# Matrix product with layer norm: the opening takes column quarter 2 of B first

## The chip, the cores and the metric

The kernel runs on one core of one Trainium2 chip. Its time is the device time of one execution in microseconds (us), median of several runs. A profile shows one execution on five engines: TensorE (PE; its weight loads are a row of their own, PEld), VectorE (DVE), ScalarE (ACT), GpSimd (POOL) and SyncE (SP), which here only issues DMA transfers, in the order of its queue. The *span* is the time from the first to the last instruction of the profiled execution.

## The reference

```python
x = np.matmul(a, b)                       # a, b: 2048 x 2048 float32
mean = np.mean(x, axis=-1, keepdims=True)
var = np.var(x, axis=-1, keepdims=True)
normalized = (x - mean) / np.sqrt(var + eps)
return (gamma * normalized + beta).astype(np.float32)
```

A matrix product whose rows are normalised and then scaled and shifted by two vectors. The kernel multiplies in fp16 and adds up in fp32.

## The kernel before, in words

**Tiles.** The output has 16 row blocks of 128 rows. Its 2048 columns are cut into four column quarters of 512; one quarter of one row block fills one of the eight PSUM banks. The inner dimension has 16 k-tiles of 128. One product is a 128x128 block of A (transposed, as the weights) by a 128x512 block of B, and there are 16 x 4 x 16 = 1024 of them, all issued by `mm` (line 85). All of B is kept in SBUF as fp16 in `b16`, k-tile by k-tile, with the four quarters side by side.

**Why there is an opening.** B comes in as float32 in the course of the kernel, so the first R = 5 row blocks are worked on together while it arrives. For these rows a quarter is not finished at once. It is summed over the k-tiles that are there, the partial sum is copied out of PSUM into the row's buffer `xs` by ScalarE (`put_aside`, line 264), and later partial sums are added to it by VectorE (`add_part`, line 268; `add_rest`, line 272, which also takes the statistics of the quarter). Three quarters are put aside early, in the order given by `ASIDE`; the fourth is `MAIN`, quarter 3.

**The order of work in the opening** is written out by hand, since the kernel is scheduled manually: each engine runs its instructions in program order.

- Loads: the list `arrivals` (line 163) interleaves five blocks of A (rows 0 to 4, k-tiles 0 to 3) and four blocks of B (`load_b1`, one k-tile of the first aside quarter each), 256 KB apiece. Then come 512 KB blocks of two k-tiles (`load_b2`): the other two aside quarters for k-tiles 0 to 3, the main quarter for k-tiles 0 to 11 mixed with more of A, then k-tiles 4 to 11 of the first aside quarter and 4 to 7 of quarter 1. All are issued by SyncE into one pool of six staging buffers and cast to fp16 by VectorE.
- Products: `filler` matmuls on zeros (line 245) keep TensorE busy until data are there; `turn` (line 247) transposes blocks of A on TensorE and copies them out with ScalarE. Then follow the first aside quarter for k-tiles 0 to 3, the second and third (line 302), the main quarter for k-tiles 0 to 11, and after that `part` for each quarter's remaining k-tiles: the first aside quarter k-tiles 4 to 11, the second and third k-tiles 4 to 15, the main one 12 to 15, and last the first aside quarter's 12 to 15.
- The rest of B's loads stand in the list `later` (line 354), cast by ScalarE. After the last load of the third aside quarter, and after the last of the list, a small GpSimd copy (`gate`, line 362) holds GpSimd's queue back, on which whole rows of A for the blocks from 5 on are loaded (`load_row`, line 343). SyncE then turns these with transposing DMAs (`turn_ahead`, line 347).
- `close_opening` (line 459) adds the very last partial sums of each opening row, works out mean and deviation (`stats`, line 100) and queues the row's normalising in two pieces, columns 0 to 1023 and 1024 to 2047 (`queue_norm`, line 130). These pieces are done by VectorE, one after each quarter of the later rows (`drain`).

**The rest.** Row blocks 5 to 15 go quarter by quarter in the order 0, 1, 2, 3, sixteen products each (`quarter`, line 449). The last row has its own ending (`finish_row`, line 400).

Of the kernel before, what the change touches and what calls it, by code (L numbers as in the profile page):

```python
# [16 lines left out]
def kernel(  # L17
# [9 lines left out]
    nc = tc.nc  # L27
    P = 128
# [4 lines left out]
    n_kt = K // P  # L33
    NB = 512
    n_nb = N // NB
    NH = N // 2
    KC = 4
    KW = KC * P
    n_kc = n_kt // KC
    R = 5  # L40
    ASIDE, MAIN = (0, 1, 2), 3
    assert n_kt % KC == 0 and n_nb == 4 and n_mt > R + 2

    if isinstance(eps, bass.AP):
# [21 lines left out]
    b16 = bpool.tile([P, n_kt, N], FP16)  # L66
# [6 lines left out]
    def bank(name):  # L73
        return psum.tile([P, NB], FP32, tag="ps", name=name)
# [4 lines left out]
    def at(i):  # L79
        return pair[i // 2][:, i % 2]  # L80

    def mm(i, q, kt, first, last):
        if (i, q) not in acc:
            acc[i, q] = bank(f"acc{i}_{q}")
        nc.tensor.matmul(  # L85
            acc[i, q], at(i)[:, kt, :], b16[:, kt, ds(q * NB, NB)],
            start=first, stop=last,
        )
# [81 lines left out]
    def half_stage():  # L170
        n = fresh["st"]
        if n % 2 == 0:
            held["st"] = stg.tile([P, 2, NB], FP32, tag="st", name=f"st{n // 2}")
        fresh["st"] += 1
        return held["st"][:, n % 2, :]
# [19 lines left out]

    def load_b1(k):
        st = half_stage()
        nc.sync.dma_start(st, b[ts(k, P), 0:NB])  # L198
        nc.vector.tensor_copy(b16[:, k, 0:NB], st)  # L199

    def load_b2(k, q, cast=nc.vector.tensor_copy):
        st = stg.tile([P, 2, NB], FP32, tag="st", name=f"stb{q}_{k}")
        nc.sync.dma_start(
            st, b[ds(k * P, 2 * P), ds(q * NB, NB)].rearrange("(t p) n -> p t n", p=P))
        cast(b16[:, k:k + 2, ds(q * NB, NB)], st)  # L205
        return st
# [3 lines left out]
    def load_pair(j, c):  # L210
        if len(pairs[j]) == 2:
            load_a2(pairs[j][0], c)
        else:
            load_a1(pairs[j][0], c)

    for what in arrivals:
        (load_a1(what[1], 0) if what[0] == "a" else load_b1(what[1]))
# [4 lines left out]
    K3 = n_kt - KC  # L222
    for c in range(n_kc - 1):
# [4 lines left out]
        if c + 2 < n_kc:  # L228
            if c > 0:
                load_pair(1, c + 1)  # L230
            load_pair(2, c + 1)
    load_b2(KC, 0)
    load_b2(KC + 2, 0)
    for j in range(len(pairs)):
        load_pair(j, n_kc - 1)
        if j < 2:
            load_b2(2 * KC + 2 * j, 0)
    load_b2(KC, 1)
    load_b2(KC + 2, 1)

# [2 lines left out]
    def filler(n, to=None):  # L243
        for _ in range(n):
            nc.tensor.matmul(warm if to is None else to, zeros[:, 0:P], zeros, start=True, stop=True)  # L245

    def turn(rows, c):
        n = len(rows)
        t_ps = psum.tile([P, n, KC, P], FP16, tag="ps", name=f"tps{rows[0]}_{c}")
        for m, i in enumerate(rows):  # L250
            for j in range(KC):
                nc.tensor.transpose(t_ps[:, m, j, :], a16_of[i, c][:, ts(j, P)], ident)  # L252
        i0 = rows[0]
        nc.scalar.copy(  # L254
            pair[i0 // 2][:, ds(i0 % 2, n), ds(c * KC, KC), :], t_ps)

    def turn_last(i):
        nc.sync.dma_start_transpose(at(i)[:, ds(K3, KC), :], a16_of[i, n_kc - 1])

    def put_aside(p, q):  # L260
        if xs[p] is None:
            xs[p] = xpool.tile([P, N], FP32, tag="x", name=f"x{p}")
            bnst[p] = stat.tile([P, n_nb, 6], FP32, tag="bnst", name=f"bnst{p}")
        nc.scalar.copy(xs[p][:, ds(q * NB, NB)], acc.pop((p, q)))  # L264
# [11 lines left out]
    filler(9)  # L276
    turn([0], 0)
    filler(3)
    mm(0, 0, 0, True, False)
    filler(1)  # L280
    turn([1], 0)
    filler(2)
    for i in range(2, R - 1):
        turn([i], 0)
        mm(i - 1, 0, 0, True, False)
    for p in range(R - 2):
        mm(p, 0, 1, False, False)
    for kt in (0, 1):
        mm(R - 2, 0, kt, kt == 0, False)
    for p in range(R - 2):  # L290
        mm(p, 0, 2, False, False)
    turn([R - 1], 0)
    mm(R - 2, 0, 2, False, False)
    for p in range(R - 1):
        mm(p, 0, 3, False, True)
        put_aside(p, 0)
    for kt in range(KC):
        mm(R - 1, 0, kt, kt == 0, kt == KC - 1)
    put_aside(R - 1, 0)


    for q in ASIDE[1:]:
# [8 lines left out]
    def part(q, k0, k1, k_row, done):  # L311

        for kt in range(k0, k_row):
            for p in range(R):
                mm(p, q, kt, kt == k0, False)
        for p in range(R):
            for kt in range(k_row, k1):
                mm(p, q, kt, kt == k0, kt == k1 - 1)
            done(p, q)
# [23 lines left out]
    def load_row(i):  # L343
        a16[i] = a16p.tile([P, K], FP16, tag="a16", name=f"a16_{i}")
        nc.gpsimd.dma_start(a16[i], a[ts(i, P), :])  # L345
# [6 lines left out]


    later = [(k, 1) for k in range(2 * KC, n_kt, 2)]
    later += [(k, 2) for k in range(KC, n_kt, 2)]
    later += [(k, q) for q in (MAIN, 0) for k in range(K3, n_kt, 2)]
    for n, (k, q) in enumerate(later):
        for i in {0: (0,), 1: (1,), 2: (2,), 4: (3, 4)}.get(n, ()):
            turn_last(i)
        st = load_b2(k, q, nc.scalar.copy)  # L360
        if (k, q) in ((n_kt - 2, 2), later[-1]):
            nc.gpsimd.tensor_copy(gate, st[:, 0, 0:1])
        if (k, q) == (n_kt - 2, 2):
            load_row(R)
    turn_ahead(R)


    part(0, KC, K3, K3 - 2, add_part)
    part(1, KC, n_kt, K3, add_rest)
    part(2, KC, n_kt, K3, add_rest)  # L370
    nc.sync.dma_start(gamma_b, gamma.unsqueeze(0).to_broadcast([P, N]))
    nc.sync.dma_start(beta_b, beta.unsqueeze(0).to_broadcast([P, N]))
    if eps_ap is not None:
# [87 lines left out]
        queue_norm(p, *stats(p))  # L461

    part(MAIN, K3, n_kt, K3, add_rest)
    part(0, K3, n_kt, K3, close_opening)
    for i in range(R, n_mt):
        last = i == n_mt - 1
        turn_ahead(i + 2)
# [49 lines left out]
```

## Time and profile before

| | |
|---|---|
| median of three runs | 244.88 us (243.92, 244.88, 245.12) |
| the profiled execution's own time | 245.38 us |
| its span, mean granted TensorE clock | 242.9 us, 0.994 |
| products (line 85) | 1024, 379 ns each in the records (they overlap), 223.0 us busy |
| VectorE casts of B | 4 of 256 KB at 0.43 us, 16 of 512 KB at 0.69 us |
| ScalarE casts of B | 14 of 512 KB at 1.04 us |
| ScalarE copies of partial sums (line 264) | 20 at 0.61 us |
| VectorE sums (lines 268, 272) | 5 and 20 at 0.68 us |
| HBM read, written | 35.67 MB, 16.78 MB |

A line of the profile names the program line and engine, the operation, the tile written and the tiles read, and the busy time. An arrow `<-` after an idle time names what ended it. The line `DMA` of the profile's slices gives the busy share of the core's 16 DMA engines in tenths in 40 equal slices of the span, and `GB/s` what they moved. A matmul's recorded duration is longer than the distance to the next one, because matmuls overlap; the distance is had from the chain of waits, which merges a run of them into one line with a count. The chain is followed back from the last instruction to what released it, and shown here in order of time.

### The profile page before, as it was taken

Reading aid. Unit: us, or ns where it says so; the run is one execution under the profiler, and the core shown is the slowest. Engines: PE = TensorE matmul, PEld = TensorE weight load, DVE = VectorE, ACT = ScalarE, POOL = GpSimd, SP = SyncE. Lnnn points to the kernel's source line nnn. Section 1 sums busy time; section 2 is a strip of 40 time slices with the busy share of each in tenths; the row PEclk is TensorE's granted clock in tenths of the full one; section 3 lists DMA queues with packets and bytes.
Section 4 is the critical chain, followed back from the end, with each engine's and each line's share of the span. In section 5 each row is a group of like instructions: output and inputs, shape, how many; then the busy total and the mean of one; then the engine's idle time right before and its main releaser. Section 6 shows DMA issues by size and latency. Waiting matters only on the chain.

```text
span 242.9 us, 2971 instructions
## 1 busy us (share of the span) xinstructions
PE 234.3 (96%) x1117; PEld 107.2 (44%) x1117; DVE 171.2 (70%) x300; ACT 65.9 (27%) x115; POOL 12.7 (5%) x20
## 2 busy tenths in 40 slices
PE   7899999999999999999999999999999999999992
PEld 2344554344444444444444444444444444444441
DVE  1543554625449998999999999998758292846761
ACT  2376444065750013020201103022111121212132
POOL 0000000000120001000000000005400000000000
PEclk9999999999999999999999999999999999999997
DMA  5999999999979999749899978988907235130405
GB/s 101 391 387 387 385 366 300 275 356 386 385 153 198 350 224 169 233 154 205 248 200 233 254 166 292 245 202 199 260 33 170 89 112 150 47 126 1 173 0 173
DMA packets 43909, 53.28 MB, mean 219 GB/s; under 512 B 27124, under 2 KB 27124, under 8 KB 43640
## 3 DMA queue, kind: packets, MB, share of 16 engines
q1 hardware_dynamic: 42312, 47.34, 62.7%
q0 software_dynamic: 1584, 5.77, 14.5%
q8 instruction: 8, 0.13, 0.2%
q14 instruction: 5, 0.04, 0.0%
HBM read 35.67 MB, written 16.78 MB: 216 GB/s over the span
## 4 chain that ended last, share of the span: by engine, by line
PE 93%; DMA 2%; DVE 1%; ACT 1%; SPq 0%; issue 0%; DVEq 0%
PE acc L85 91%; DMA st<-in_a_dram 2%; PE tps L252 1%; ACT x L442 1%; DVE x L268 1%; DVE bnst L407 0%; PE y L430 0%; DVE a16s L186 0%; PE warm L245 0%; SPq L198 0%; SPq L184 0%; PE ms_ps L425 0%; ACT mv_last L423 0%; DVE mv_last L422 0%; ACT lead L426 0%
## 5 line engine op out<-in xcount | busy, mean ns | idle before, releaser
L85 PE MATMUL acc<-b,at 128*128 128x512 f16 x1024 | 223.0, 379 | 1.5 <-DVE b L199 1.0
L85 PEld LDWEIGHTS <-at 128*128 128x128 f16 x1024 | 99.7, 98 | 120.5 <-issue 1.2
L96 DVE BATCH_NORM_STATS2 bnst<-x 128x6 f32<-128x512 f32 x43 | 29.5, 689 | 23.4 <-ACT x L95 23.4
L117 DVE SCALAR_TENSOR_TENSOR x<-x,rstd,beta_b 128x512 f32<-128x512 f32 x62 | 43.9, 748 | 0.6
L111 DVE SCALAR_TENSOR_TENSOR x<-x,mv,gamma_b 128x512 f32<-128x512 f32 x60 | 43.1, 760 | 0.0
L95 ACT COPY x<-acc 128x512 f32<-128x512 f32 x43 | 24.5, 585 | 66.9 <-PE acc L85 66.7
L272 DVE TENSOR_TENSOR x<-acc,x 128x512 f32<-128x512 f32 x20 | 13.6, 678 | 13.4 <-PE acc L85 13.4
L106 ACT ACTIVATE sq<-ve 128x1 f32<-128x1 f32 x15 | 3.0, 203 | 65.8 <-DVE ve L104 65.8
L205 DVE CAST b<-stb 128x1024 f16<-128x1024 f32 x16 | 11.1, 694 | 13.1 <-DMA stb<-in_b_dram 13.1
L205 ACT CAST b<-stb 128x1024 f16<-128x1024 f32 x14 | 14.6, 1045 | 16.6 <-DMA stb<-in_b_dram 16.6
L273 DVE BATCH_NORM_STATS2 bnst<-x 128x6 f32<-128x512 f32 x20 | 13.9, 694 | 0.7
L264 ACT COPY x<-acc 128x512 f32<-128x512 f32 x20 | 10.2, 610 | 5.7 <-PE acc L85 5.7
L254 ACT COPY at<-tps 128x512 f16<-128x512 f16 (+1 forms) x11 | 8.0, 741 | 13.1 <-PE tps L252 12.9
L345 POOL DMA_DIRECT2D a<-in_a_dram x11 | 6.0, 545 | 92.8 <-DMA at<-a 92.0
L245 PE MATMUL warm<-zeros 128*128 128x512 f16 x19 | 6.5, 476 | 1.2 <-DVE zeros L152 1.2
L186 DVE CAST a16s<-st 128x512 f16<-128x512 f32 x8 | 3.4, 428 | 5.7 <-DMA st<-in_a_dram 5.6
L194 DVE CAST a16s<-sta 128x1024 f16<-128x1024 f32 x6 | 4.2, 694 | 4.1 <-DMA sta<-in_a_dram 4.1
L391 POOL TENSOR_SCALAR gb<-gb 1x1024 f32<-1x1024 f32 x2 | 5.8, 2917 | 0.0
L252 PE MATMUL tps<-ident,a16s 128*128 128x128 f16 x60 | 5.2, 220 | 0.6 <-DVE a16s L186 0.6
L252 PEld LDWEIGHTS <-a16s 128*128 128x128 f16 x60 | 3.9, 98 | 3.9 <-DVE a16s L186 2.2
L102 DVE BATCH_NORM_AGGREGATE mv<-bnst 128x2 f32<-128x24 f32 x15 | 4.0, 264 | 0.5
L245 PEld LDWEIGHTS <-zeros 128*128 128x128 f16 x19 | 2.1, 118 | 4.4 <-issue 2.9
(33 smaller groups left out, 26.3 us busy)
## 6 DMA issues: line engine op xcount, KB each, us to landing
stb<-in_b_dram SPq DMA_DIRECT2D x30, 512.0 KB, 6.8
out_dram<-x SPq DMA_DIRECT2D x30, 512.0 KB, 3.3
a<-in_a_dram POOLq DMA_DIRECT2D x11, 512.0 KB, 6.2
sta<-in_a_dram SPq DMA_DIRECT2D x6, 512.0 KB, 6.5
st<-in_a_dram SPq DMA_DIRECT2D x8, 256.0 KB, 6.5
st<-in_b_dram SPq DMA_DIRECT2D x4, 256.0 KB, 6.6
gamma_b<-in_gamma_dram SPq DMA_DIRECT2D x1, 1024.0 KB, 5.5
beta_b<-in_beta_dram SPq DMA_DIRECT2D x1, 1024.0 KB, 8.3
```

Source lines behind the costliest of these rows:

```text
L85: nc.tensor.matmul(acc[i, q], at(i)[:, kt, :], b16[:, kt, ds(q * NB, NB)], start=first, stop=last,)
L95: nc.scalar.copy(xs[i][:, qs], acc[i, q])
L96: nc.vector.bn_stats(bnst[i][:, q, :], xs[i][:, qs])
L111: nc.vector.scalar_tensor_tensor(xs[i][:, qs], xs[i][:, qs], mv[:, 0:1], gamma_b[:, qs], AluOp.subtract, AluOp.mult)
L117: nc.vector.scalar_tensor_tensor(xs[i][:, qs], xs[i][:, qs], rstd, beta_b[:, qs], AluOp.mult, AluOp.add)
L205: cast(b16[:, k:k + 2, ds(q * NB, NB)], st)
L245: nc.tensor.matmul(warm if to is None else to, zeros[:, 0:P], zeros, start=True, stop=True)
L252: nc.tensor.transpose(t_ps[:, m, j, :], a16_of[i, c][:, ts(j, P)], ident)
L254: nc.scalar.copy(pair[i0 // 2][:, ds(i0 % 2, n), ds(c * KC, KC), :], t_ps)
L264: nc.scalar.copy(xs[p][:, ds(q * NB, NB)], acc.pop((p, q)))
L272: nc.vector.tensor_tensor(xs[p][:, qs], acc[p, q], xs[p][:, qs], AluOp.add)
L273: nc.vector.bn_stats(bnst[p][:, q, :], xs[p][:, qs])
```

## The change

`ASIDE` is turned round from (0, 1, 2) to (2, 1, 0), and a name `Q0` for its first entry replaces the literal 0 wherever the first aside quarter was meant; `ASIDE[2]` replaces the literal 2 in the same way. So in the five opening rows quarter 2 of B is loaded, multiplied and put aside first and closed last, and quarter 0 takes the place that quarter 2 had. Quarters 1 and 3 stay where they were, and so do all rows from 5 on. The four loads of `load_b1` now read columns 1024 to 1535 of B.

```diff
-    ASIDE, MAIN = (0, 1, 2), 3
+    ASIDE, MAIN = (2, 1, 0), 3
+    Q0 = ASIDE[0]
...
     def load_b1(k):
         st = half_stage()
-        nc.sync.dma_start(st, b[ts(k, P), 0:NB])
-        nc.vector.tensor_copy(b16[:, k, 0:NB], st)
+        qs = ds(Q0 * NB, NB)
+        nc.sync.dma_start(st, b[ts(k, P), qs])
+        nc.vector.tensor_copy(b16[:, k, qs], st)
...
-    load_b2(KC, 0)
-    load_b2(KC + 2, 0)
+    load_b2(KC, Q0)
+    load_b2(KC + 2, Q0)
...
-            load_b2(2 * KC + 2 * j, 0)
+            load_b2(2 * KC + 2 * j, Q0)
...
-    mm(0, 0, 0, True, False)
+    mm(0, Q0, 0, True, False)
...
     for p in range(R - 1):
-        mm(p, 0, 3, False, True)
-        put_aside(p, 0)
+        mm(p, Q0, 3, False, True)
+        put_aside(p, Q0)
...
-    later += [(k, 2) for k in range(KC, n_kt, 2)]
-    later += [(k, q) for q in (MAIN, 0) for k in range(K3, n_kt, 2)]
+    later += [(k, ASIDE[2]) for k in range(KC, n_kt, 2)]
+    later += [(k, q) for q in (MAIN, Q0) for k in range(K3, n_kt, 2)]
...
-        if (k, q) in ((n_kt - 2, 2), later[-1]):
+        if (k, q) in ((n_kt - 2, ASIDE[2]), later[-1]):
             nc.gpsimd.tensor_copy(gate, st[:, 0, 0:1])
-        if (k, q) == (n_kt - 2, 2):
+        if (k, q) == (n_kt - 2, ASIDE[2]):
             load_row(R)
...
-    part(0, KC, K3, K3 - 2, add_part)
+    part(Q0, KC, K3, K3 - 2, add_part)
     part(1, KC, n_kt, K3, add_rest)
-    part(2, KC, n_kt, K3, add_rest)
+    part(ASIDE[2], KC, n_kt, K3, add_rest)
...
     part(MAIN, K3, n_kt, K3, add_rest)
-    part(0, K3, n_kt, K3, close_opening)
+    part(Q0, K3, n_kt, K3, close_opening)
```

More of the change, by code (lines that the diff above doesn't have):

```diff
@@ L284 @@
         turn([i], 0)
-        mm(i - 1, 0, 0, True, False)
+        mm(i - 1, Q0, 0, True, False)
     for p in range(R - 2):
-        mm(p, 0, 1, False, False)
+        mm(p, Q0, 1, False, False)
     for kt in (0, 1):
-        mm(R - 2, 0, kt, kt == 0, False)
+        mm(R - 2, Q0, kt, kt == 0, False)
     for p in range(R - 2):
-        mm(p, 0, 2, False, False)
+        mm(p, Q0, 2, False, False)
     turn([R - 1], 0)
-    mm(R - 2, 0, 2, False, False)
+    mm(R - 2, Q0, 2, False, False)
     for p in range(R - 1):
-        mm(p, 0, 3, False, True)
-        put_aside(p, 0)
+        mm(p, Q0, 3, False, True)
+        put_aside(p, Q0)
     for kt in range(KC):
-        mm(R - 1, 0, kt, kt == 0, kt == KC - 1)
-    put_aside(R - 1, 0)
+        mm(R - 1, Q0, kt, kt == 0, kt == KC - 1)
+    put_aside(R - 1, Q0)
     for q in ASIDE[1:]:
```

## The prediction

> **What bounds the kernel now.** I read the page first (busy shares, slices, chain), then the chain in order of time, TensorE's own waits, the timeline of the opening, and DMA rates microsecond by microsecond. The page:
>
> ```profile
> span 242.9 us, 2971 instructions
> PE 234.3 (96%) x1117; PEld 107.2 (44%) x1117; DVE 171.2 (70%) x300; ACT 65.9 (27%) x115; POOL 12.7 (5%) x20
> ...
> PE 93%; DMA 2%; DVE 1%; ACT 1%; SPq 0%; issue 0%; DVEq 0%
> ```
>
> TensorE is busy 96% of the span and makes 93% of the chain that ended last. The chain in order of time (start, duration, what) shows whether it runs without holes:
>
> ```profile
> 1.66 6.00 DMA st<-in_a_dram
> ...
> 9.25 0.39 PE acc L85
> ...
> 12.31 12.73 PE acc L85 x59
> ...
> 46.84 1.29 DVE x L268 x2
> ...
> 48.17 185.79 PE acc L85 x860
> ```
>
> 59 matmuls in 12.73 us are 0.2158 us each, 860 in 185.79 us are 0.2160: one rate over nearly the whole kernel. What TensorE waits for, totalled (us, times, longest):
>
> ```profile
> PE warm L245 <- DVE zeros L152: 1.2, 1, 1.2
> PE acc L85 <- DVE b L199: 1.0, 1, 1.0
> PE tps L252 <- DVE a16s L186: 0.6, 1, 0.6
> PE acc L85 <- DVE x L268: 0.4, 2, 0.2
> ```
>
> Three of these lie in the first 9 us; the last is the 0.4 us at 47 us, where `add_part` gives PSUM banks back. So the time is the opening (9.24 us to the second product), a stream at a fixed rate to 233.97 us, and an 8.9 us tail. A change that keeps the products can act only on the opening, on the stream by opening a hole, or on the tail. In the opening the data come late:
>
> ```profile
> 4.92 0.43 DVE L186 CAST a16s<-st 128x512 f16<-128x512 f32 x1 [3.71 <-DMA st<-in_a_dram]
> 7.01 0.43 DVE L199 CAST b<-st 128x512 f16<-128x512 f32 x1 [1.67 <-DMA st<-in_b_dram]
> 7.69 0.43 DVE L186 CAST a16s<-st 128x512 f16<-128x512 f32 x1 [0.25 <-DMA st<-in_a_dram]
> 8.36 0.43 DVE L186 CAST a16s<-st 128x512 f16<-128x512 f32 x1 [0.25 <-DMA st<-in_a_dram]
> ```
>
> A's first block is cast at 4.92, B's first at 7.01, then one 256 KB block each 0.67 us. The gap of 2.09 us before B's first block is 1.42 us over that pace. The rates (window, length, busy time by engine, clock, DMA share, GB/s):
>
> ```profile
> 2.00:3.00 1.00, 1.00 (x4) 0.43 (x3) 0.00 (x0) 0.02 (x1) 0.00 (x0) 1.00 0.56 190
> 3.00:4.00 1.00, 1.00 (x4) 0.33 (x3) 0.00 (x0) 0.00 (x0) 0.00 (x0) 1.00 0.66 102
> 4.00:5.00 1.00, 0.84 (x3) 0.15 (x1) 0.08 (x1) 0.00 (x0) 0.00 (x0) 1.00 0.91 100
> 5.00:6.00 1.00, 0.59 (x6) 0.43 (x7) 0.35 (x1) 0.16 (x1) 0.00 (x0) 1.00 0.82 176
> 7.00:8.00 1.00, 0.51 (x2) 0.10 (x1) 0.74 (x2) 0.00 (x0) 0.00 (x0) 1.00 1.05 404
> ```
>
> Reads crawl at about 100 GB/s from 3 to 5 us and run at 404 from 7 on. This slow spell is the only place where an address might matter, and the whole question of this case.
>
> **The change part by part.** It renames: in the order of column quarters 2 and 0 change places. I go through what is moved.
>
> *The four first B loads (`load_b1`).* Before and after: four SyncE DMAs of 256 KB, 128 rows of 2048 bytes with 8192 bytes between rows, each followed by a VectorE cast of 0.43 us. Number, size, place in SyncE's queue and in VectorE's order stay; only the start in each row moves from byte 0 to byte 4096. Cost 4 x (0.43 - 0.43) = 0, if the DMA takes as long. No row shows quarter 2 read first, so I bound it: from below by the whole spell vanishing (3 to 6 us moved 102 + 100 + 176 = 378 KB, which at 404 GB/s takes 0.94 us, so -2.06 us), from above by B's first block losing its 1.42 us once more (+1.42). I take 0, by the nearest rows: the blocks cast from 7.69 on come from the same bytes 0 to 2047 of their rows as the two slow ones, and run at the full pace.
>
> *The 512 KB loads (`load_b2`).* The groups for quarter 2 (2 in the opening, 6 in the later list) now read quarter 0 and the other way round (4 and 2, besides the 4 small loads). Casts of 512 KB blocks in the opening follow one another at 13.08, 14.44 (quarter 1), 15.78, 17.14 (quarter 2) and 18.50 (A): 1.36, 1.34, 1.36, 1.36 us, so quarters 1 and 2 and A cost the same. Quarter 0's own small blocks ran at 0.67 us per 256 KB, the same rate again. VectorE casts of 0.69 us and ScalarE casts of 1.04 us stay as many and in the same places, 16 and 14. Cost 0. The cover is thin at the start: B's fourth block is cast from 11.71 to 12.14, and the first product that needs it starts at about 12.37 (one product after 12.15), so 0.2 us is hidden; the first 512 KB block is ready at 13.77 and wanted 8 products later at about 14.1, so 0.3 us. Any delay beyond that goes one for one into the end. In the later list the cover is wide: the block for k-tile 8 of quarter 1 is ready at 49.5 and wanted after 60 products from 47 us, about 60 us; quarter 2's last block is ready at 61.3 and wanted after 68 us.
>
> *The products (`mm`), 80 of quarter 0 and 80 of quarter 2 in the five opening rows.* Same number, same weights, same order of k-tiles and rows, other columns of `b16`. All matmuls of the group last 376 to 389 ns in the records whichever quarter they read, and the spacing is 0.216 us throughout. Cost 0.
>
> *Evacuations and sums (`put_aside`, `add_part`, `add_rest`).* Same engines, same count (ScalarE 20 x 0.61, VectorE 5 x 0.68 and 20 x 0.68 with 20 x 0.69 of statistics), another 2 KB of each row of `xs`. Cost 0.
>
> *The gate copies and the row load behind them.* They follow the third aside quarter and the last load of the list, by place as before: the GpSimd copies (0.18 us) and the first whole-row load on its queue keep their place, and so does the transpose on SyncE behind it. Cost 0.
>
> *The close of the opening rows.* The last quarter that `close_opening` sums is now 2. The work queued behind it begins with columns 0 and 1; that used to follow a fresh sum of quarter 0 and now follows a fresh sum of quarter 2. VectorE runs both in its own order, and between the sum and the first centring (L111, 93.92 us) lie the statistics of all rows (from 84.1 to 92.6), so nothing waits for it. The normalising, its stores and rows 5 to 15 are not touched, nor is the tail. Cost 0; no wait is added anywhere.
>
> Sum 0. The profiled execution took 245.38 us, of which 242.9 are the span and 2.48 lie around it; the median of the three runs is 244.88, 0.50 below it (0.2%). I forecast no change, 244.9 us against the median.
>
> **The rivals.** *The slow spell belongs to the columns (faster).* A's and B's first blocks read bytes 0 to 2047 of rows 0 to 127 of two matrices of the same 16 MB; the two might stand in each other's way, and after the change B's stands 4096 bytes off. Then B's first block lands 0.67 us after A's, at 5.57 instead of 7.0, and each block behind it is 1.42 us earlier. TensorE would follow: the first product could start when the transposed A is copied out (6.42), and the second turn behind it and one filler at about 6.9, against 8.17; the blocks after that hold it back, and they are 1.42 us earlier. Time 244.88 - 1.42 = 243.46; with the whole spell gone 242.8. For it: the spell hits these two blocks. Against it: A's first block was complete at 4.92, so from 5 us on these two no longer meet, and yet 5 to 6 us moves only 176; from 7 on blocks of A and B with the same columns mix at 404. It looks like the age of the kernel or a first contact with the memory, which the change leaves. [...] Chance 0.12.
>
> *The new columns read slowly where the old did not (slower).* Quarter 2 of B's rows meets A's stream or something else at the start, and B's first block loses its 1.42 us a second time. Place: the same gap before the first B cast, at 7 us now. Everything behind it on SyncE's one queue lands later and TensorE with it, because the cover above is only 0.2 us; it decides by the 0.5% from a delay of about 1.4 us on (1.2 us and the cover). Time 244.88 + 1.42 = 246.30. Against it: quarter 2's blocks at 15.78 and 17.14 came at the common pace beside A's. Chance 0.10.
>
> *Waits by span instead of by piece (slower).* A 512 KB cast writes two k-tiles, with other quarters lying between its two pieces. If the program's waits were set by the whole span, the products of k-tile 1 on quarter 2 would wait for the cast of quarter 3, done at 19.85 + 0.69 = 20.54, about 10 us late: 255. Against it: the same span covers k-tile 1 of quarter 0 today, and those products run in the nine from 9.92 us on, before even the first such cast at 13.08. Chance 0.02.
>
> **How the numbers follow.** No change has 0.76: same instructions, same order, same sizes, and full pace from every quarter wherever a row shows it. About 0.5% (1.2 us) is what a measurement of this kernel can tell from no change: the three runs alone spread from 243.92 to 245.12. Of the 0.76 I give 0.01 to each side for that spread. Faster 0.12 + 0.01 = 0.13; slower 0.10 + 0.02 + 0.01 = 0.13; same 0.74. The range reaches from the faster rival's 243.4 to the slower rival's 246.3; the far ends (242.8 and 255) stay out. The forecast's own range is 243.9 to 245.4, the lowest run and the profiled one.
>
> **What would show it.** Right: the casts of A's first and B's first block stand about 2.1 us apart, with about 100 GB/s from 3 to 5 us; 0.67 us between the following casts; 860 products in one piece at 0.216 us; TensorE's waits the same four lines; the last products end near 234 us; the tail 8.9 us. The faster rival shows as a gap of about 0.7 us before the first B cast and a second turn near 6.9 us; the slower as a gap of 3.5 us; the third as a new TensorE wait of 10 us on a VectorE cast of `b` (L205). I am wrong if the first reads depend on their columns, or if a quarter's place in SBUF changes a cast's or a product's duration, which no row hints at.

## The result, and the profile after

The changed kernel took 245.94 us (median of 17 runs, 245.08 to 247.50), the kernel before 244.31 us in as many runs beside it (243.61 to 245.44). The ratio is 1.0069, with a 95% interval of 1.0049 to 1.0089: slower by 1.6 us, a little over the 0.5% that the prediction set as the limit of what can be told. The profiled execution took 245.94 us, with a span of 243.8.

The page of the changed kernel:

```profile
span 243.8 us, 2971 instructions
PE 235.4 (97%) x1117; PEld 107.9 (44%) x1117; DVE 171.2 (70%) x300; ACT 65.9 (27%) x115; POOL 12.7 (5%) x20
...
PE 91%; DMA 4%; SPq 1%; ACT 1%; DVE 1%; issue 0%
```

The number of instructions is the same to the last one and so is the busy time of every engine but TensorE. In the chain, DMA has gone from 2% to 4%. In order of time (start, duration, what) it reads:

```profile
4.02 8.80 DMA st<-in_a_dram
...
13.73 0.22 PE acc L86
...
13.96 12.68 PE acc L86 x58
26.64 0.45 PE tps L254 x8
...
34.70 200.12 PE acc L86 x927
```

The first DMA link of the chain now ends at 12.82 us, with A's fifth block, where it ended at 7.66 with A's second. The unbroken run of products begins at 13.96, where a run longer by one product began at 12.31. The two runs are best compared by their ends, at the next transposes (`tps`). In the kernel before these stand at 25.05, and the products behind the last of them start at 33.11:

```profile
25.05 0.45 PE tps L252 x8
...
33.11 13.61 PE acc L85 x63
```

So TensorE is 1.59 us late at both places (26.64 and 34.70). After that the rate is what it was: 927 products in 200.12 us are 0.2159 us each. TensorE's own waits (us, times, longest) agree:

```profile
PE acc L86 <- DVE b L201: 1.8, 2, 1.0
PE warm L247 <- DVE zeros L153: 1.2, 1, 1.2
PE y L432 <- ACT lead L428: 0.4, 1, 0.4
```

The wait for a cast of B's small blocks has grown from 1.0 to 1.8 us, in two pieces. Where the blocks are late shows in VectorE's casts of the nine 256 KB blocks, which are the first casts of all (start, duration, what, and in brackets the idle time before and what ended it):

```profile
3.96 0.43 DVE L187 CAST a16s<-st 128x512 f16<-128x512 f32 x1 [2.75 <-DMA st<-in_a_dram]
5.28 0.43 DVE L201 CAST b<-st 128x512 f16<-128x512 f32 x1 [0.90 <-DMA st<-in_b_dram]
5.94 0.43 DVE L187 CAST a16s<-st 128x512 f16<-128x512 f32 x1 [0.23 <-DMA st<-in_a_dram]
7.40 0.43 DVE L187 CAST a16s<-st 128x512 f16<-128x512 f32 x1 [1.03 <-DMA st<-in_a_dram]
8.30 0.43 DVE L187 CAST a16s<-st 128x512 f16<-128x512 f32 x1 [0.48 <-DMA st<-in_a_dram]
9.70 0.43 DVE L201 CAST b<-st 128x512 f16<-128x512 f32 x1 [0.97 <-DMA st<-in_b_dram]
11.98 0.43 DVE L201 CAST b<-st 128x512 f16<-128x512 f32 x1 [1.86 <-DMA st<-in_b_dram]
12.85 0.43 DVE L187 CAST a16s<-st 128x512 f16<-128x512 f32 x1 [0.44 <-DMA st<-in_a_dram]
13.48 0.43 DVE L201 CAST b<-st 128x512 f16<-128x512 f32 x1 [0.21 <-DMA st<-in_b_dram]
```

Before, one gap was long (2.09 us, ahead of B's first block) and all others were 0.65 to 0.68. Now the first A block comes 0.96 us earlier and B's first block 1.73 us earlier, and then the train stumbles at five of the blocks behind: over the pace of 0.67 us a block, the eight gaps add up to 13.48 - 3.96 - 8 x 0.67 = 4.16 us, where they added up to 11.71 - 4.92 - 8 x 0.67 = 1.43 before. So the ninth block comes 4.16 - 1.43 - 0.96 = 1.77 us later (13.48 against 11.71), and TensorE is 1.59 us late. The rates (window, length, busy time by engine, clock, DMA share, GB/s) show the same:

```profile
3.00:4.00 1.00, 1.00 (x4) 0.33 (x3) 0.04 (x1) 0.00 (x0) 0.00 (x0) 1.00 0.92 299
5.00:6.00 1.00, 1.00 (x7) 0.71 (x6) 0.49 (x2) 0.32 (x1) 0.00 (x0) 1.00 0.82 190
7.00:8.00 1.00, 1.00 (x9) 0.52 (x8) 0.43 (x1) 0.24 (x1) 0.00 (x0) 1.00 0.85 256
```

Three times the rate of before in the fourth microsecond, but 256 GB/s where it had reached 404.

The two profiled spans differ by only 0.9 us, since the execution profiled before had a hole at 47 us: the four products from 46.72 to 48.17 took 1.45 us instead of 4 x 0.216 = 0.86, because `add_part` came late. The changed kernel, 1.59 us later by then (34.70 against 33.11), does not have it. So 1.59 - 0.59 = 1.00, and the last product ends 0.85 us later (234.82 against 233.97; the remaining 0.15 is the slightly shorter spacing). The tail is 8.9 us before and 9.0 after.

### The profile page after: what moved, and what is told of

It is laid out like the page before. It is cut to its first block, busy times and chain, and to the rows that moved or that the text cites. A ratio compares the mean times of both kernels' runs of the same rounds, so it can differ in the third digit from the quotient of the medians.

```text
span 243.8 us, 2971 instructions
## 1 busy us (share of the span) xinstructions
PE 235.4 (97%) x1117; PEld 107.9 (44%) x1117; DVE 171.2 (70%) x300; ACT 65.9 (27%) x115; POOL 12.7 (5%) x20
## 4 chain that ended last, share of the span: by engine, by line
PE 91%; DMA 4%; SPq 1%; ACT 1%; DVE 1%; issue 0%
PE acc L86 90%; DMA st<-in_a_dram 4%; PE tps L254 1%; ACT x L444 1%; SPq L185 1%; SPq L200 1%; DVE bnst L409 0%; PE y L432 0%; DVE a16s L187 0%; PE ms_ps L427 0%; ACT mv_last L425 0%; DVE mv_last L424 0%; ACT lead L428 0%
## 5 line engine op out<-in xcount | busy, mean ns | idle before, releaser
L207 DVE CAST b<-stb 128x1024 f16<-128x1024 f32 x16 | 11.1, 694 | 12.9 <-DMA stb<-in_b_dram 12.9
L207 ACT CAST b<-stb 128x1024 f16<-128x1024 f32 x14 | 14.6, 1045 | 15.9 <-DMA stb<-in_b_dram 15.9
L256 ACT COPY at<-tps 128x512 f16<-128x512 f16 (+1 forms) x11 | 8.1, 741 | 14.5 <-PE tps L254 14.5
L247 PE MATMUL warm<-zeros 128*128 128x512 f16 x19 | 7.5, 539 | 1.2 <-DVE zeros L153 1.2
L201 DVE CAST b<-st 128x512 f16<-128x512 f32 x4 | 1.7, 427 | 3.9 <-DMA st<-in_b_dram 3.9
```

Source lines behind the costliest of these rows:

```text
L256: nc.scalar.copy(pair[i0 // 2][:, ds(i0 % 2, n), ds(c * KC, KC), :], t_ps)
```

## The experiments

All experiments were timed in the same rounds as the kernel before, and each ratio is to its runs in those rounds (medians of 244.11 to 244.39 us; the row "before" has those of the result). "A at" and "B at" are the byte in a row at which the small first blocks begin; the pitch of the rows of A and of B is 8192 bytes. The casts are those of the profiled execution.

| kernel | A at | B at | first A cast | fourth B cast | median, us | ratio to before, 95% interval |
|---|---|---|---|---|---|---|
| before | 0 | 0 | 4.92 | 11.71 | 244.31 | |
| changed | 0 | 4096 | 3.96 | 13.48 | 245.94 | 1.0069 [1.0049, 1.0089] |
| e1 | 0 | 4096 | 3.97 | 13.60 | 245.85 | 1.0061 [1.0036, 1.0087] |
| e2 | 0 | 0 | 5.10 | 11.55 | 244.06 | 0.9999 [0.9979, 1.0019] |
| e3 | 4096 | 0 | 4.11 | 12.06 | 245.43 | 1.0050 [1.0018, 1.0083] |
| e4 | 4096 | 4096 | 4.82 | 11.09 | 244.41 | 1.0005 [0.9981, 1.0028] |
| e5 | 0 | 0, then 4096 | 4.98 | 12.19 | 244.89 | 1.0022 [1.0002, 1.0041] |
| e6 | 0 | 4096, then 0 | 3.95 | 11.60 | 244.43 | 0.9995 [0.9974, 1.0017] |
| e7 | 0 | 2048 | 4.18 | 11.47 | 244.56 | 1.0007 [0.9983, 1.0030] |
| e8 | 0 | 6144 | 3.93 | 11.72 | 244.28 | 0.9994 [0.9973, 1.0016] |
| e9 | 2048 | 6144 | 4.10 | 12.07 | 245.95 | 1.0067 [1.0040, 1.0094] |
| e10 | 0 | 4096, other rows | 4.02 | 11.37 | 245.34 | 1.0029 [1.0006, 1.0052] |
| e11 | 0 | 0, late | 7.74 | 14.12 | 248.05 | 1.0139 [1.0111, 1.0167] |
| e12 | 0 | 4096, late | 7.06 | 15.20 | 247.72 | 1.0120 [1.0093, 1.0146] |

A profile is one draw. The profiled executions of e3 and e10 (both 244.39 us) were the second fastest of their twelve and that of e7 (243.81) the fastest, so their casts are on the good side; that of e1 (247.72) was the slowest of its twelve. What a distance costs is therefore read from the medians, and the casts show only the pattern.

**Is it the address in HBM?** The change moves two things: where the small loads read in HBM and where they write in SBUF, together with the order of everything behind. e1 takes the kernel before and moves the HBM address alone; e2 takes the changed kernel and puts the HBM address alone back.

```diff
 e1, in load_b1 of the kernel before:
-        nc.sync.dma_start(st, b[ts(k, P), 0:NB])
+        nc.sync.dma_start(st, b[ts(k, P), 2 * NB:3 * NB])
 e2, in load_b1 of the changed kernel:
-        nc.sync.dma_start(st, b[ts(k, P), qs])
+        nc.sync.dma_start(st, b[ts(k, P), 0:NB])
```

> The kernel before, but its four small B loads fetch columns 1024 to 1535 from HBM; everything else, the place in SBUF too, is as before. It leaves the product of k-tiles 0 to 3 with quarter 0 wrong: the columns of quarter 2 stand in for it. Theory 1 (the address in HBM of the first B reads makes the opening's transfers slow): slower by the whole difference, about 1.6 us (245.9 against 244.3), with A's fifth block cast at about 12.8 us instead of 11.05. Rival (the place in SBUF, the order of the later loads or of the products does it): the time of before, 244.3, and the cast at 11.05.

> The changed kernel, but its four small B loads fetch columns 0 to 511 from HBM, into the place of quarter 2. It leaves the product of k-tiles 0 to 3 with quarter 2 wrong: the columns of quarter 0 stand in for it. Theory 1 (address in HBM of the first B reads): back to the time of before, 244.3, with A's fifth block cast near 11.05 us. Rival (place in SBUF, order of the later loads or of the products): stays at 245.9 with that cast near 12.8.

e1 is as slow as the change (1.0061), e2 as fast as before (0.9999). The casts of e1 follow those of the changed kernel closely (5.28, 5.94, 7.40 and 11.98 there):

```profile
5.29 0.43 DVE L199 CAST b<-st 128x512 f16<-128x512 f32 x1 [0.89 <-DMA st<-in_b_dram]
5.93 0.43 DVE L186 CAST a16s<-st 128x512 f16<-128x512 f32 x1 [0.22 <-DMA st<-in_a_dram]
7.60 0.43 DVE L186 CAST a16s<-st 128x512 f16<-128x512 f32 x1 [1.25 <-DMA st<-in_a_dram]
...
11.95 0.43 DVE L199 CAST b<-st 128x512 f16<-128x512 f32 x1 [2.14 <-DMA st<-in_b_dram]
```

So the start addresses of the four 256 KB loads are the whole cost; the place in SBUF, the order of the later loads, the products and the close are free, as the prediction priced them, to within e2's interval of 0.2% (0.5 us) either way.

**Is it B's address or its distance to A's?** e3 moves A's five small blocks by 4096 bytes and leaves B; e4 moves both.

```diff
 e3 and e4, in load_a1 of the kernel before:
-        nc.sync.dma_start(st, a[ts(i, P), ts(c, KW)])
+        nc.sync.dma_start(st, a[ts(i, P), ts(c if c else 2, KW)])
 e4 also, in load_b1:
-        nc.sync.dma_start(st, b[ts(k, P), 0:NB])
+        nc.sync.dma_start(st, b[ts(k, P), 2 * NB:3 * NB])
```

> The kernel before, but the five first A blocks fetch columns 1024 to 1535 of A instead of 0 to 511, so it is A's reads that move by 4096 bytes and B's that stay. It leaves k-tiles 0 to 3 of the five opening rows wrong: k-tiles 8 to 11 of A stand in for them. If the distance between the columns of A and B is what counts: slower by about 1.6 us, like the change. If B's own address counts: the time of before, 244.3.

> The kernel before with both moves: the first A blocks and the four small B loads fetch columns 1024 to 1535. It leaves the first four k-tiles of the opening rows wrong for A, and quarter 0 of k-tiles 0 to 3 wrong for B. If the distance between the columns of A and B counts: both lie 4096 bytes on, the distance is 0 again, the time of before, 244.3. If B's own address counts: slower by about 1.6 us, 245.9.

The distance counts: A moved alone costs (1.0050, interval 1.0018 to 1.0083), both moved cost nothing (1.0005). e4's casts have the pattern of before, one long gap and then the pace:

```profile
4.82 0.43 DVE L186 CAST a16s<-st 128x512 f16<-128x512 f32 x1 [3.61 <-DMA st<-in_a_dram]
6.34 0.43 DVE L199 CAST b<-st 128x512 f16<-128x512 f32 x1 [1.09 <-DMA st<-in_b_dram]
7.03 0.43 DVE L186 CAST a16s<-st 128x512 f16<-128x512 f32 x1 [0.26 <-DMA st<-in_a_dram]
7.70 0.43 DVE L186 CAST a16s<-st 128x512 f16<-128x512 f32 x1 [0.25 <-DMA st<-in_a_dram]
```

**Which distances, and which blocks?** My second theory was that the 16 DMA engines collide at the start whenever they read equal columns, that this sorts them into an order that holds, and that any other distance gives weaker but longer collisions. e5 and e6 mix the distances among the four B blocks, e7 and e8 take the two other quarters.

```diff
 load_b1 of the kernel before, in e5, e6, e7 and e8:
-        nc.sync.dma_start(st, b[ts(k, P), 0:NB])
+        nc.sync.dma_start(st, b[ts(k, P), ds((0 if k == 0 else 2) * NB, NB)])   # e5
+        nc.sync.dma_start(st, b[ts(k, P), ds((2 if k == 0 else 0) * NB, NB)])   # e6
+        nc.sync.dma_start(st, b[ts(k, P), NB:2 * NB])                           # e7
+        nc.sync.dma_start(st, b[ts(k, P), 3 * NB:4 * NB])                       # e8
```

> The kernel before, but of the four small B loads the first fetches columns 0 to 511 as before and the other three fetch columns 1024 to 1535. It leaves the product of k-tiles 1 to 3 with quarter 0 wrong: quarter 2's columns stand in. Theory 2 (the 16 DMA engines collide at the start on equal columns, and the collision sorts them into an order that then holds; once sorted, other columns do no harm): the time of before, 244.1, slow until about 5.5 us, then 0.67 us a block. Rival A (any change of columns between neighbouring blocks in the first 12 us costs): most of the change's cost stays, 245.3 or more, with the blocks after the fourth late.

> The complement: the first small B load fetches columns 1024 to 1535, the other three columns 0 to 511 as before. It leaves the product of k-tile 0 with quarter 0 wrong: quarter 2's columns stand in. Theory 2 (the first blocks sort the engines): the early rate is near 270 GB/s from 3 to 5 us as after the change; the sorting then happens over the blocks of equal columns behind, a1 to b1, so that it ends between before and after, 244.1 to 245.3. Rival A (every change of columns costs): two changes (before and behind the first B block) of the five that the changed kernel has, so 244.1 + 2/5 x 1.6 = 244.8, with blocks from the fifth on at 0.67 us.

> The kernel before, its four small B loads fetching columns 512 to 1023, 2048 bytes off A's. It leaves the product of k-tiles 0 to 3 with quarter 0 wrong: quarter 1's columns stand in. Theory 2: any other columns than A's give weaker and longer collisions, so about 245.7, and A's fifth block cast later than 12 us. Rival B (4096 bytes is a special distance): the time of before, 244.1, and that cast at 11.

> The kernel before, its four small B loads fetching columns 1536 to 2047, 6144 bytes off A's. It leaves the product of k-tiles 0 to 3 with quarter 0 wrong: quarter 3's columns stand in. Theory 2: about 245.7, and A's fifth block cast later than 12 us. Rival B (4096 bytes is a special distance): the time of before, 244.1, and that cast at 11.

The second theory falls with e7 and e8: 2048 and 6144 bytes cost nothing that their intervals can tell (1.0007 and 0.9994, at most 1.0030 and 1.0016). They are not free of stumbles; e7's first blocks show one, but it does not go on:

```profile
5.18 0.43 DVE L199 CAST b<-st 128x512 f16<-128x512 f32 x1 [0.57 <-DMA st<-in_b_dram]
6.80 0.43 DVE L186 CAST a16s<-st 128x512 f16<-128x512 f32 x1 [1.20 <-DMA st<-in_a_dram]
7.89 0.43 DVE L186 CAST a16s<-st 128x512 f16<-128x512 f32 x1 [0.66 <-DMA st<-in_a_dram]
8.53 0.43 DVE L186 CAST a16s<-st 128x512 f16<-128x512 f32 x1 [0.22 <-DMA st<-in_a_dram]
```

Its gaps 5.18 to 6.80 and 6.80 to 7.89 are 0.95 and 0.42 us over the pace. Over all eight gaps e7 loses 11.47 - 4.18 - 5.36 = 1.93 us, the kernel before 1.43, but e7's first A block is 0.74 us earlier, so the ninth block comes at about the same time. A single B block at 4096 costs nothing either (e6: 0.9995), three cost about a third by the medians (e5: 1.0022, interval 1.0002 to 1.0041), where the first rival had wanted 245.3 or more and got 244.89. In e5 the one late block is A's fifth, between two B blocks at 4096:

```profile
9.86 0.43 DVE L199 CAST b<-st 128x512 f16<-128x512 f32 x1 [0.18 <-DMA st<-in_b_dram]
11.54 0.43 DVE L186 CAST a16s<-st 128x512 f16<-128x512 f32 x1 [1.26 <-DMA st<-in_a_dram]
12.19 0.43 DVE L199 CAST b<-st 128x512 f16<-128x512 f32 x1 [0.22 <-DMA st<-in_b_dram]
```

So every pattern pays for some stumble, 0.9 to 2.4 us over the nine blocks in the kernels that are no slower and in e5 (e4: 11.09 - 4.82 - 5.36 = 0.91; e8: 11.72 - 3.93 - 5.36 = 2.43), and those without equal columns at the very front get up to 1 us of it back by an earlier first block. At 4096 bytes on all blocks it went on to 4.2 us in the changed kernel and 4.3 in e1. In e3, a good draw, it was 2.6, little more than in e8, so there the cost is shown by the median alone. In e9, which follows, it was 2.6 as well, and more was added behind it.

**Does it hold elsewhere?** The third theory: blocks 4096 bytes apart in their rows collide, wherever they lie. e9 tries the pair 2048 and 6144, e10 takes B's blocks from rows 1024 on.

```diff
 e9, in load_a1 and load_b1 of the kernel before:
-        nc.sync.dma_start(st, a[ts(i, P), ts(c, KW)])
+        nc.sync.dma_start(st, a[ts(i, P), ts(c if c else 1, KW)])
-        nc.sync.dma_start(st, b[ts(k, P), 0:NB])
+        nc.sync.dma_start(st, b[ts(k, P), 3 * NB:4 * NB])
 e10, in load_b1:
-        nc.sync.dma_start(st, b[ts(k, P), 0:NB])
+        nc.sync.dma_start(st, b[ts(k + 8, P), 2 * NB:3 * NB])
```

> The kernel before, but the five first A blocks fetch columns 512 to 1023 (byte 2048 on) and the four small B loads columns 1536 to 2047 (byte 6144 on): other columns than in the change, the same distance of 4096 bytes. It leaves the opening rows' first four k-tiles wrong for A, and quarter 0 of k-tiles 0 to 3 wrong for B. Theory 3 (blocks of A and B 4096 bytes apart in their rows collide at the start, wherever they lie): slower like the change, 245.7 to 246. Rival (the pair of bytes 0 and 4096 alone): the time of before, 244.3.

> The kernel before, its four small B loads fetching columns 1024 to 1535 of rows 1024 to 1535 instead of rows 0 to 511. It leaves the product of k-tiles 0 to 3 with quarter 0 wrong: another part of B stands in. Theory 3 (the distance within the row counts, not which rows): slower like the change, 245.7 to 246. Rival (A and B collide because their blocks also have the same or near row numbers): the time of before, 244.3.

e9 costs as much as the change (1.0067), so the distance counts and not the pair of columns. Its profile shows a second way in which late blocks can cost: the fourth B cast was only 0.36 us later than before (12.07), but TensorE lost its clock meanwhile (windows as above, the clock is the third figure from the end):

```profile
10.00:11.00 1.00, 0.79 (x3) 0.29 (x3) 0.58 (x2) 0.06 (x1) 0.00 (x0) 0.84 0.94 309
11.00:12.00 1.00, 1.00 (x4) 0.43 (x3) 0.43 (x1) 0.00 (x0) 0.00 (x0) 0.50 1.02 352
12.00:13.00 1.00, 1.00 (x4) 0.33 (x3) 0.43 (x1) 0.00 (x0) 0.00 (x0) 0.50 1.05 406
13.00:14.00 1.00, 1.00 (x6) 0.58 (x5) 0.59 (x1) 0.18 (x1) 0.00 (x0) 0.50 1.06 410
```

TensorE's own timeline has eight products in that time:

```profile
10.21 3.15 PE L85 MATMUL acc<-b,at 128*128 128x512 f16 x8 [0.56 <-DVE b L199]
```

The same eight took 1.89 us in e3, at a clock of 1.00, which is 1.26 us less; here the run of products began only at 13.78. By the runs' mean clocks the lost clock is not all of e9's cost: eight of its twelve runs had a mean clock of 0.990 to 0.996, where the kernel before has 0.989 to 0.996, and still took 245.41 to 246.96 us. e10 lies between (1.0029, interval 1.0006 to 1.0052): it costs, but less than the change by their medians, so the row numbers may matter too; this was not settled.

**Is it the start of the kernel?** In the prediction I took the slow spell from 3 to 5 us for the age of the kernel. e11 and e12 put two 512 KB loads ahead, in the kernel before and in the changed one.

```diff
 e11 and e12, in the two kernels:
+    load_b2(0, 1)
+    load_b2(2, 1)
     for what in arrivals:
...
-    for q in ASIDE[1:]:
-        load_b2(0, q)
-        load_b2(2, q)
+    load_b2(0, ASIDE[2])
+    load_b2(2, ASIDE[2])
```

> The kernel before with two 512 KB loads of the opening (quarter 1, k-tiles 0 to 3) moved to the very front of SyncE's queue, so that A's first block starts about 3 us later. Slower than before by about 2.7 us (two blocks of 1.35 us), 247.0, by every theory; it is the partner of the next run.

> The changed kernel with the same two loads moved to the front. If the collisions belong to the first microseconds of transfers, and A's and B's blocks are free of them once others have run ahead: equal to its partner with quarter 0 first, 247.0, within 0.3%. If A and B blocks of 256 KB collide at 4096 bytes at any time: slower than the partner by about 1.6 us, 248.6.

The spell moves with the blocks. e11 reads at 264 and 397 GB/s from 3 to 5 us, where the kernel before crawled, and crawls when A's and B's first blocks come, from 6 to 8 us, where e12 with its distance of 4096 reads at 336 and 389:

```profile
3.00:4.00 1.00, 1.00 (x4) 0.33 (x3) 0.00 (x0) 0.00 (x0) 0.00 (x0) 1.00 0.89 264
4.00:5.00 1.00, 1.00 (x3) 0.15 (x1) 0.19 (x1) 0.00 (x0) 0.00 (x0) 1.00 1.03 397
...
6.00:7.00 1.00, 0.00 (x0) 0.00 (x0) 0.69 (x1) 0.00 (x0) 0.00 (x0) 1.00 0.96 143
7.00:8.00 1.00, 0.00 (x0) 0.00 (x0) 0.26 (x1) 0.00 (x0) 0.00 (x0) 1.00 0.76 127
```

And in e12 the stumbles of the 4096 distance come as well, at 12 to 14.5 us:

```profile
10.92 0.43 DVE L201 CAST b<-st 128x512 f16<-128x512 f32 x1 [0.25 <-DMA st<-in_b_dram]
12.37 0.43 DVE L201 CAST b<-st 128x512 f16<-128x512 f32 x1 [1.02 <-DMA st<-in_b_dram]
14.50 0.43 DVE L187 CAST a16s<-st 128x512 f16<-128x512 f32 x1 [1.71 <-DMA st<-in_a_dram]
```

So neither belongs to the first microseconds, as far as a shift by 3 us can tell. The times of the two cannot tell more: they are equal within their spread (247.69 to 248.95 and 247.07 to 248.16, six runs each), though e12's fourth B block is 1.08 us later, because in e11 TensorE was itself late. After 3.0 us without work (5.2 to 8.2 us) its fillers and first products were spaced 0.43 us until about 12.5:

```profile
8.22 0.61 PE L253 MATMUL tps<-ident,a16s 128*128 128x128 f16 x4 [3.01 <-DVE a16s L186]
8.62 1.49 PE L246 MATMUL warm<-zeros 128*128 128x512 f16 x3
```

The run of products started at 15.69, though the fourth B cast was done at 14.55; that of e12 started at 15.68. It fits e11's miss too: 247.0 was expected from the two blocks alone, and it took 248.05. By its expectation e12 would speak for a collision of the start alone; by the traces it does not.

## Why the prediction was right or wrong

**What was right.** The range of 243.4 to 246.3 held the measured 245.94, but in part by luck: its upper end was the median of three runs, 244.88, plus 1.42, while the 17 runs put the kernel before at 244.31, and from there the measured 1.63 us is more than 1.42. The forecast itself, no change with a chance of 0.74, did not come: the interval of the ratio, 1.0049 to 1.0089, leaves 1 out. The sum over the edits was right in every term but one: e2, which has all of the change except the four read addresses, takes the time of before. The cover of 0.2 us at B's fourth block was right too: a delay of 1.77 us there left TensorE 1.59 late. The rate of 0.216 us, the tail and the order of the rest stayed.

**What was wrong: the first term, "the four first B loads", taken as 0.** The step bounded it by -2.06 and +1.42 and took 0 "by the nearest rows", which showed blocks of equal columns at full pace and, later, 512 KB blocks of other columns at full pace. Neither row had a 256 KB block 4096 bytes away from its neighbour, and that is what the change makes. It measured 1.77 us at the fourth B cast in the profiled pair and 1.6 us in the medians. Both are above the upper bound, which allowed for one late block, where five blocks behind B's first came late.

**The slower rival** was the case that came, at 0.10: 246.30 forecast, 245.94 measured. Its place was wrong. It had B's first block lose 1.42 us more; in fact that block came 1.73 us earlier, and the seven blocks behind it took 13.48 - 5.28 = 8.20 us instead of 4.70. "Against it: quarter 2's blocks at 15.78 and 17.14 came at the common pace" was an argument from another kind of block.

**The faster rival** had half of the mechanism. The spell does belong to the columns: in the four kernels without loads ahead whose first blocks of A and B have equal columns (before, e2, e4, e5) the reads from 3 to 5 us run at 98 to 131 GB/s, in the other eight at 238 to 313, but for e7's 133 in the second of these microseconds. It is not the kernel's age (e11). My argument against it, that 5 to 6 us moves only 176 although A's first block was complete by then, was wrong: the changed kernel, without the spell, moved 190 in that microsecond. The gain came as well, 1.73 us at B's first block, and was then given back twice over (8.20 - 4.70 = 3.50). The Trainium skill, "DMA: Bandwidth & Descriptors", section on latency and other measured facts, says that copies of rows at a pitch of 4 MiB ran at 103 GB/s, and at full rate, 214, with the pitch padded by 4 KiB. Here a shift of 4 KiB between two streams at 8 KiB pitch is the bad one (1.0050 to 1.0069 in four kernels), and 2 or 6 KiB are harmless (1.0007, 0.9994); the page speaks of the pitch of rows, not of a shift between two tensors, and its cure does not carry over.

**The rival of waits by span** did not come: no wait of TensorE names a cast of a 512 KB block (L207); of B's casts it waits only for the small ones (L201).

**What stays open.** That the cost lies in the reads from HBM, and in the 4096 bytes between the places of neighbouring small blocks of A and B in their rows, is shown by the times. Why that distance, and whether channels or banks of the memory are hit, is not: no trace names them, nor where A and B lie in memory, so a distance here is one within the row and not between addresses. Whether the row numbers matter (e10) is open too. Nor was it tried why the 512 KB blocks behind, where A at byte 2048 and quarter 3 at byte 6144 stand side by side, keep a pace of 1.31 to 1.36 us in both kernels (before from 13.08 to 21.20 us, after from 14.82 to 22.79). No version here beats the kernel before.

## What to carry to other kernels

Two interleaved load streams are not independent of each other: before a load is moved to other columns, compare its offset within a row with those of its neighbours in the queue, and where no row of the trace has that very pair of block size and offset, keep the whole bound in the forecast. To find which part of a renaming costs, move the source address alone and then everything but the source address; two such kernels settled here what no reasoning from the old trace could. In an opening whose loads are hidden by 0.2 us, a late last block reaches the end almost whole (1.77 us late, TensorE 1.59).

## What the hardware showed that I had not expected

- A shift of 4096 bytes between two streams of 256 KB blocks, rows 8192 bytes apart, cost 1.3 to 1.7 us (1.0050 to 1.0069) in the four kernels that had it on all blocks with the same rows; shifts of 0, 2048 and 6144 bytes cost nothing that could be measured.
- With equal columns there is one long gap, ahead of B's first block (0.85 to 1.42 us over the pace in before, e2, e4 and e11), and then 0.63 to 0.73 us a block; the kernel before read at 102 and 100 GB/s from 3 to 5 us, the changed one at 299 in the first of the two. A fast start was no sign of a fast train.
- The granted TensorE clock fell to 0.50 for some three microseconds in e9 (11 to 14 us) though no gap of TensorE in the six microseconds ahead was longer than 0.96 us; in the changed kernel, with gaps of 0.73 and 1.05 us, it stayed at 1.00.
- The clock figure of a window is not the whole story: from 9 to 11 us e11 and e12 both space their fillers about 0.43 us apart, and the windows show 1.00 in e11 and 0.50 in e12.
